# Experts of at most 64 tokens: both parts of the activations side by side in one weight tile, and a block's places by one instruction

## The chip, the cores and the metric

The kernel runs on one core of one Trainium2 chip. The metric is the device time of one execution in microseconds (us), given as the median of several runs. In the profile the engines are PE (TensorE, the matrix products), PEld (TensorE loading its weights, which overlaps PE), DVE (VectorE), ACT (ScalarE), POOL (GpSimd) and SP (SyncE, which issues most transfers). Matrix results land in PSUM, in banks of 128 rows by 512 float32; everything else is in SBUF.

## What is computed

The program is two blocks of a network on 512 tokens of 1024 features, all in float32. The change touches one stage of the first block, the mixture of experts:

```python
expert_id = grp_idx * EXPERTS_PER_GROUP + top_idx      # two of 16 experts per token
for e in range(N_EXPERTS):
    h = jax.nn.silu(t @ w_e_gate[e]) * (t @ w_e_up[e])  # 1024 -> 512
    y = y + comb[:, e:e + 1] * (h @ w_e_down[e])        # 512 -> 1024
```

The 512 tokens choose 1024 places in all, so an expert has 64 tokens on average; how many it has depends on the inputs.

## The kernel before

**Experts in an order.** The kernel computes only the tokens that chose an expert. It sorts 14 of the 16 experts by size at run time and works on them in a fixed order of places e = 0 to 15. `RANKS` (line 62) gives the rank by size that stands at each place, and `SIZES` (line 63) the rows that a block of each rank gets: places 0 to 4 have 128 rows, 5 and 6 have 96, 7 and 8 have 80, 9, 10, 12 and 13 have 64, 14 and 15 have 48. Places 4 and 11 (`DOUBLE`) have a second block of 128 rows that shares the weights: 18 blocks in all.

**Float32 by three passes.** TensorE takes float32 here in an exact split, a high part and a low part. `mm3` (line 519) makes a term of a product by three passes: high by high, high by low, low by high. In the experts the activations are the stationary operand (128 features by the block's rows) and the weights stream past, 512 columns a pass. Each pass has its own line: 522 (high activations, high weights), 523 (high activations, low weights), 524 (low activations, high weights).

```python
mm(ps, lhsT=lhsT[0], rhs=rhs[0], start=first, stop=False)
mm(ps, lhsT=lhsT[0], rhs=rhs[1], start=False, stop=False)
mm(ps, lhsT=lhsT[1], rhs=rhs[0], start=False, stop=last)
```

**Weights.** An expert has 12 chunks of 128 by 1024 weights (512 KB), four each for gate, up and down. `Stream` loads them ahead from SP (line 213), ScalarE copies the high part (`whi`, line 275), and VectorE subtracts to get the low part (`wlo`, line 283). One chunk in twelve, and a few more, have the low part made by GpSimd (`pool_lo`). There are four pairs of tiles for parts, so the split runs at most three chunks ahead of the products. After the products of a chunk, `advance` (line 318) issues the split of the chunk three places on.

**One step of the loop (line 1958).** For expert e the order on TensorE is: gate of e (`rows_mm`, 8 terms, one bank), down of e - 1 (`down`, 4 terms by two banks), up of e (`rows_mm`, 8 terms). A block thus takes 24 + 24 + 24 = 72 passes. Beside them:
- `hidden` (line 1659), after the up product: ScalarE takes silu of the gate's bank (line 1663), VectorE multiplies it with the up bank (line 1664).
- `next_h`, in the next gate: the hidden rows are transposed (line 1331) and split by `parts_T` (line 1628), high part by ScalarE (line 1638), low part by VectorE (line 1639), into two tiles `hl`. `next_x`, in the up phase, does the same with the gathered tokens of the next expert.
- at the end of `down` (line 1667), ScalarE copies each of two banks to `ye` (line 1689), GpSimd multiplies by a row, `gt_f` (line 1690), and GpSimd issues the transfer to memory (line 1692). The last expert's two banks are multiplied by VectorE straight from PSUM instead (line 1687), and SP sends the rows.
- in chunk 0 of the up phase, `pre_prep` makes the one-hot matrix of the block two blocks on: `one_hots` (line 1527) compares a row of 0, 1, 2, ... with the tokens' places, one instruction for each of four tiles of tokens (line 1531). In chunk 3, `prep` turns it into a list of tokens and gathers their rows by an indirect transfer from GpSimd (line 1548).

Each engine takes its instructions in the order in which they are issued here. `first_max`, `order`, `places` and the norm of a memory tensor (`memory_parts`) run as tasks beside the products, in the same queues. After the last `down` the rows are gathered back (line 2057) and a second norm and the second block follow; that part is not changed.

Of the kernel before, what the change touches and what calls it, by code (L numbers as in the profile page):

```python
# [20 lines left out]
NT = 4  # L21
# [19 lines left out]
# The experts in the order of their work: two stand still, and the two largest of the others come  # L41
# at places where two blocks of tokens share the weights.
# [17 lines left out]
# By the place in that order: the rank by size of its expert, and the rows of its (first) block. Of  # L60
# the others, the k-th largest has 1024 / k tokens at most; what is beyond a block is computed too.
RANKS = (-1, -1, 2, 3, 0, 4, 5, 6, 7, 8, 9, 1, 10, 11, 12, 13)
SIZES = (128, 128, 128, 128, 96, 96, 80, 80, 64, 64, 64, 64, 48, 48)
# [102 lines left out]
class Stream:  # L166
    """Chunks of weights in the order of their use: loads run ahead, then each chunk is cut
    exactly into a high and a low part of float32r."""
# [90 lines left out]
    def prepare(self):  # L259
        """What is done first to the chunks that are loaded."""  # L260
# [3 lines left out]
    def split_hi(self):  # L264
        """The high part of the next chunk."""
# [12 lines left out]
    def split_lo(self):  # L278
        """The low part, after the high one."""
# [28 lines left out]
    def take_raw(self, key):  # L308
        """A chunk as it is."""
# [8 lines left out]
    def advance(self, late=False):  # L318
        """Called after the products of a chunk: the parts of a later one."""
# [15 lines left out]
class Steps:  # L335
    """Instructions that depend on one another, put in the order in which the engines could start
    them: an engine takes its instructions in the order of their emission."""
# [6 lines left out]
    def add(self, engine, us, fn, deps=(), at=0.0, late=0.0):  # L344
        """us: about how long it holds its engine; at: not before; late: gives way to others."""
# [31 lines left out]
class Kern:  # L377
# [49 lines left out]
    def act_view(self, act, q, h):  # L427
        """Tiles 4h .. 4h + 3 of a part as one tile [128, 4, 512]."""
# [17 lines left out]
    def rsqrt(self, out, in_, premul, eps, n, p=128):  # L446
        """out = (in_ * premul + eps) ** -0.5 by Newton's steps from a guess of the exponent."""
# [30 lines left out]
    def steps_rsqrt(self, steps, z, dep, scale, eps, h0, late=0.0):  # L478
        """(z["ss"] * scale + eps) ** -0.5 of [128, 1] in z["r"], in steps after dep."""
# [21 lines left out]
    def log1p_exp_neg_abs(self, out, x, n, p=128):  # L501
        """out = log(1 + exp(-|x|)), by the series of the inverse hyperbolic tangent."""
# [16 lines left out]
    def mm3(self, ps, lhsT, rhs, first, last):  # L519
        """One term of a float32 product: three passes over exact parts."""  # L520
# [5 lines left out]
    def proj_T(self, ps, w, m0, act, nk, k0=0, every=0):  # L526
        """ps[128 features, 512 tokens] = w[:, :, m0:m0+128].T @ act, over nk tiles of rows."""
# [7 lines left out]
    def step(self, n=1):  # L535
        """Emit the next part of every task that runs beside the products."""
# [144 lines left out]
    def times_gt(self, t, n):  # L681
        """The columns of the mix's last product times 1 + gt_m."""
# [5 lines left out]
    def row_tiles(self, names):  # L688
        """The four tiles of rows [128, 1024]."""
# [3 lines left out]
    def first_mixer(self):  # L693
# [18 lines left out]
        # silu(c)  # L712
# [6 lines left out]
        # normalised x, transposed  # L719
# [27 lines left out]
        # the first two modulations by feature, a half of each by products, a half by sums  # L747
# [83 lines left out]
        # block-diagonal weights of the gates  # L831
# [20 lines left out]
        # ---- forget gates: cum of log_sigmoid along the tokens, rows of heads  # L852
# [5 lines left out]
        def forget(ps):  # L858
# [19 lines left out]
            # sums along the tokens, rows of heads  # L878
# [17 lines left out]
        # ---- recurrent branch  # L896
# [65 lines left out]
        # squares summed over the features, by half; the scales of their rows  # L962
# [3 lines left out]
        def mixed(nm, m, src, hl):  # L966
            """Tile m of a half of the features is ready."""
# [32 lines left out]
        # ---- attention, two heads after the others  # L1000
# [31 lines left out]
        # ---- the projections  # L1032
# [60 lines left out]
        # the experts' rows; those of blocks that may not be computed are cleared  # L1093
# [37 lines left out]
        # the experts' rows; those of blocks that may not be computed are cleared  # L1131
# [2089 lines left out]
```

## Time and profile before

| what | value |
|---|---|
| time before, median of 3 runs | 2381.77 us (2377.67 to 2387.61) |
| profiled execution: span, first to last instruction | 2380.5 us |
| own time of the profiled execution | none is given beside its span |
| PE busy | 2253.2 us (95%) |
| DVE busy | 1494.7 us (63%) |
| ACT busy | 1164.1 us (49%) |
| POOL busy | 435.0 us (18%) |
| stage of the experts, first pass to last | 380.7 to 745.3 us |

The span is a profile of one execution. Matrix passes are pipelined: a pass of 512 columns is shown as about 400 ns long, but the next one starts some 230 ns later, so the busy time of PE counts overlaps once and hides short waits. The pace of passes is read from their starts.

### The profile page before, as it was taken

Reading aid. Unit: us, or ns where it says so; the run is one execution under the profiler, and the core shown is the slowest. Engines: PE = TensorE matmul, PEld = TensorE weight load, DVE = VectorE, ACT = ScalarE, POOL = GpSimd, SP = SyncE. Lnnn points to the kernel's source line nnn. Section 1 sums busy time; section 2 is a strip of 40 time slices with the busy share of each in tenths; the row PEclk is TensorE's granted clock in tenths of the full one; section 3 lists DMA queues with packets and bytes.
Section 4 is the critical chain, followed back from the end, with each engine's and each line's share of the span. In section 5 each row is a group of like instructions: output and inputs, shape, how many; then the busy total and the mean of one; then the engine's idle time right before and its main releaser. Section 6 shows DMA issues by size and latency. Waiting matters only on the chain.

```text
span 2380.5 us, 29945 instructions
## 1 busy us (share of the span) xinstructions
PE 2253.2 (95%) x10972; PEld 1765.8 (74%) x10972; DVE 1494.7 (63%) x2536; ACT 1164.1 (49%) x2018; POOL 435.0 (18%) x341
## 2 busy tenths in 40 slices
PE   7789787998997899999999999999999999999998
PEld 4566466775665777778888888888777788888887
DVE  7845677989887855546567665256554566666623
ACT  5565444766675654444354443246544435444421
POOL 2464323444444411100000000011110000000000
PEclk9999897998999899999999999999999999999999
DMA  9553237989988332213333333222321232333331
GB/s 298 157 177 99 98 115 257 357 302 300 312 279 267 90 91 78 87 56 100 95 89 98 97 98 112 92 86 83 94 87 53 83 115 71 106 98 98 107 97 62
DMA packets 298091, 323.77 MB, mean 136 GB/s; under 512 B 10976, under 2 KB 216816, under 8 KB 297936
## 3 DMA queue, kind: packets, MB, share of 16 engines
q1 hardware_dynamic: 285904, 281.77, 37.5%
q0 software_dynamic: 12032, 40.00, 5.1%
q8 instruction: 88, 1.44, 0.3%
q14 instruction: 67, 0.55, 0.1%
HBM read 305.15 MB, written 16.52 MB: 135 GB/s over the span
## 4 chain that ended last, share of the span: by engine, by line
PE 62%; DVE 4%; ACT 2%; issue 1%; DMA 0%; DVEq 0%; ACTq 0%; POOLq 0%
PE ps L522 19%; PE ps L524 18%; PE ps L523 18%; PE ps L2398 2%; PE ps L2564 1%; PE ps L591 1%; PE ps L2582 1%; DVE wlo L283 1%; ACT g L2977 1%; PE ps L2563 1%; PE ps L2683 1%; DVE st L494 0%; DVE x L2956 0%; DMA y<-y_d,si 0%; PE ps L2528 0%
## 5 line engine op out<-in xcount | busy, mean ns | idle before, releaser
L283 DVE TENSOR_TENSOR wlo<-wraw,whi 128x1024 fp32r<-128x1024 f32 (+1 forms) x337 | 430.6, 1281 | 351.0 <-ACT whi L275 180.8
L522 PE MATMUL ps<-hT,whi 128*128 128x512 f32 x1280 | 514.4, 402 | 0.0
L524 PE MATMUL ps<-hT,wlo 128*128 128x512 f32 x1280 | 499.7, 390 | 0.0
L523 PE MATMUL ps<-hT,whi 128*128 128x512 f32 x1280 | 499.3, 390 | 0.0
L275 ACT ACTIVATE whi<-wraw 128x1024 fp32r<-128x1024 f32 (+1 forms) x346 | 360.2, 1048 | 212.5 <-DVE wlo L283 146.7
L522 PEld LDWEIGHTS ps<-hT,whi 128*128 128x128 f32 x1280 | 240.3, 188 | 63.7 <-issue 7.4
L524 PEld LDWEIGHTS ps<-hT,wlo 128*128 128x128 f32 x1280 | 240.2, 188 | 52.2
L523 PEld LDWEIGHTS ps<-hT,whi 128*128 128x128 f32 x1280 | 240.6, 188 | 45.6
L522 PE MATMUL ps<-whi,hi 128*128 128x512 f32 x480 | 189.5, 395 | 0.0
L524 PE MATMUL ps<-whi,lo 128*128 128x512 f32 x480 | 189.1, 394 | 0.0
L523 PE MATMUL ps<-wlo,hi 128*128 128x512 f32 x480 | 189.0, 394 | 0.0
L523 PE MATMUL ps<-wlo,hl 128*128 128x512 f32 (+4 forms) x432 | 175.6, 406 | 9.7 <-DVE wlo L283 4.9
L522 PE MATMUL ps<-whi,hl 128*128 128x512 f32 (+4 forms) x432 | 177.7, 411 | 0.4 <-ACT hl L1638 0.4
L524 PE MATMUL ps<-whi,hl 128*128 128x512 f32 (+4 forms) x432 | 173.8, 402 | 2.5 <-DVE hl L1639 2.5
L283 DVE TENSOR_TENSOR wlo<-wx,whi 128x1024 fp32r<-128x1024 f32 x107 | 147.0, 1396 | 15.2 <-ACT whi L275 13.2
L275 ACT ACTIVATE whi<-wx 128x1024 fp32r<-128x1024 f32 x121 | 125.7, 1057 | 40.4 <-PE ps L523 27.3
L596 ACT ACTIVATE gr<-ps 128x256 fp32r<-128x256 f32 (+2 forms) x128 | 49.1, 384 | 182.0 <-PE ps L591 181.4
L599 DVE TENSOR_TENSOR gr<-ps,gr 128x256 fp32r<-128x256 f32 (+2 forms) x128 | 53.9, 421 | 119.6 <-ACT gr L596 119.1
L524 PEld LDWEIGHTS ps<-whi,lo 128*128 128x128 f32 x480 | 90.1, 188 | 21.3
L523 PEld LDWEIGHTS ps<-wlo,hi 128*128 128x128 f32 x480 | 90.2, 188 | 21.0
L522 PEld LDWEIGHTS ps<-whi,hi 128*128 128x128 f32 x480 | 90.1, 188 | 20.9
L523 PEld LDWEIGHTS ps<-wlo,hl 128*128 128x128 f32 (+4 forms) x432 | 71.7, 166 | 45.8 <-DVE wlo L283 10.9
(509 smaller groups left out, 3993.7 us busy)
## 6 DMA issues: line engine op xcount, KB each, us to landing
wraw<-in_w_in_dram SPq DMA_DIRECT2D x108, 512.0 KB, 3.9
wraw<-in_w_up_dram SPq DMA_DIRECT2D x88, 512.0 KB, 3.8
wx<-in_w_e_down_dram SPq DMA_DIRECT2D x46, 512.0 KB, 4.9
wraw<-in_w_down_dram SPq DMA_DIRECT2D x44, 512.0 KB, 3.6
wx<-in_w_e_gate_dram SPq DMA_DIRECT2D x39, 512.0 KB, 5.5
wx<-in_w_e_up_dram SPq DMA_DIRECT2D x36, 512.0 KB, 6.9
ada<-in_w_ada_dram SPq DMA_DIRECT2D x32, 512.0 KB, 4.8
wraw<-in_w_e_up_dram SPq DMA_DIRECT2D x28, 512.0 KB, 8.1
```

The source lines that it names most:

```text
L275: self.k.nc.scalar.activation(out=hi[:, 0:n_el], in_=t[:, 0:n_el], func=AF.Copy)
L283: eng.tensor_tensor(out=lo[:, 0:n_el], in0=t[:, 0:n_el], in1=hi[:, 0:n_el].bitcast(F32), op=OP.subtract)
L522: mm(ps, lhsT=lhsT[0], rhs=rhs[0], start=first, stop=False)
L523: mm(ps, lhsT=lhsT[0], rhs=rhs[1], start=False, stop=False)
L524: mm(ps, lhsT=lhsT[1], rhs=rhs[0], start=False, stop=last)
L591: nc.tensor.transpose(pt_ps[:, c * 128:(c + 1) * 128], p[:, c * 128:(c + 1) * 128], self.const("ident"))
L596: nc.scalar.activation(out=hi, in_=pt_ps[:, 0:n], func=AF.Copy)
L599: nc.vector.tensor_tensor(out=lo, in0=pt_ps[:, 0:n], in1=hi.bitcast(F32), op=OP.subtract)
L2398: self.nc.tensor.matmul(ps[q][:, c], lhsT=ws[q][w][:, k, :], rhs=act()[t][k][:, c], start=(j == 0 and k == 0), stop=(j == 2 and k == KD - 1))
L2563: nc.tensor.matmul(ps, lhsT=q[e][:, c], rhs=view(k[e]), start=True, stop=False)
L2564: nc.tensor.matmul(ps, lhsT=q[e][a, c], rhs=view(k[2])[a], start=False, stop=True)
L2582: nc.tensor.matmul(ps[:, 128 * c:128 * c + 128], lhsT=lhs(view)(q, i)[64 * e:64 * e + 64], rhs=view(k, s_)[64 * e:64 * e + 64], start=True ...
```

## The change

- Ranks 12 and 13 get 64 rows in place of 48, so that places 9, 10, 12, 13, 14 and 15 all have exactly 64 rows (`PACKED`).
- For a block of 64 rows `parts_T` writes the low part beside the high part, into columns 64 to 127 of one tile of 128. `term` then takes two passes in place of three: the whole tile of 128 columns by the high weights (the results of the high part land in rows 0 to 63 of the bank, those of the low part in rows 64 to 127), and its first 64 columns by the low weights (into rows 0 to 63). The first term issues the wide pass first, the others issue it second.
- The two halves of a bank are added by `folded`: ScalarE copies rows 64 to 127 to SBUF, VectorE adds rows 0 to 63. That is done for the gate's bank, the up bank and the two banks of `down`.
- The gate of a packed expert is folded and put through silu (`gated`) in chunk 1 of the `down` between its gate and its up phase; for other experts silu stays after the up phase.
- `one_hots` makes the four tiles by one tensor_tensor with broadcast operands, in place of four tensor_scalar.

Comments were also taken out; that changes no instruction. The diff, cut to its core:

```diff
-SIZES = (128, 128, 128, 128, 96, 96, 80, 80, 64, 64, 64, 64, 48, 48)
+SIZES = (128, 128, 128, 128, 96, 96, 80, 80, 64, 64, 64, 64, 64, 64)
+PACKED = 64
...
-            for i in range(NT):
-                v.tensor_scalar(t[:, i, :], self.const("iota")[:, 0:n], col_of(i), None,
-                                op0=OP.is_equal)
+            v.tensor_tensor(out=t, in0=self.const("iota")[:, None, 0:n].to_broadcast([128, NT, n]),
+                            in1=col_of().to_broadcast([128, NT, n]), op=OP.is_equal)
...
+            if packed:
+                to = [hl[0][:, :, 0:r], hl[0][:, :, r:2 * r]]
...
+        def term(ps, x, k, w, first, last):
+            if len(x) > 1:
+                self.mm3(ps, [p[:, k, :] for p in x], w, first, last)
+                return
+            mm = nc.tensor.matmul
+            if first:
+                mm(ps, lhsT=x[0][:, k, :], rhs=w[0], start=True, stop=False)
+            mm(ps[0:PACKED], lhsT=x[0][:, k, 0:PACKED], rhs=w[1], start=False, stop=False)
+            if not first:
+                mm(ps, lhsT=x[0][:, k, :], rhs=w[0], start=False, stop=last)
...
+        def folded(ps, out=None):
+            t = self.g()[0:PACKED] if out is None else out
+            nc.scalar.activation(out=t, in_=ps[PACKED:2 * PACKED], func=AF.Copy)
+            v.tensor_tensor(out=t, in0=ps[0:PACKED], in1=t, op=OP.add)
+            return t
...
+        def gated(pg, packed):
+            if packed:
+                sg = folded(pg)
+                nc.scalar.activation(out=sg, in_=sg, func=AF.Silu)
+                return sg
...
+        def hidden(sg, pu, packed=False):
+            h = folded(pu) if packed else self.g()[0:int(pu.shape[0])]
+            v.tensor_tensor(out=h, in0=sg, in1=h if packed else pu, op=OP.mult)
...
+                if c == 1 and mid is not None:
+                    mid()
...
+                    if two:
+                        folded(py[n], ye[:, c])
+                    if at_end:
+                        v.tensor_tensor(out=ye[:, c], in0=ye[:, c] if two else py[n], in1=gt[:, c],
+                                        op=OP.mult)
```

## Rows read from the trace of the kernel before

**Rows 1.** The page's first line: the span.
```profile
span 2380.5 us, 29945 instructions
```

**Rows 2.** Busy time by stretch, one row for an expert's gate, down, up: e3, e9 to e14.
```profile
core 0: us, PE busy (x) PEld busy (x) DVE busy (x) ACT busy (x) POOL busy (x), PEclk, DMA share, GB/s
439.07:459.38 20.31, 19.64 (x101) 15.79 (x100) 19.88 (x25) 16.21 (x21) 9.48 (x5) 1.00 1.02 377
...
580.91:602.98 22.07, 19.89 (x90) 11.47 (x88) 19.57 (x21) 14.90 (x20) 11.95 (x6) 0.92 0.95 340
602.98:623.80 20.82, 19.82 (x101) 11.84 (x100) 19.44 (x25) 16.00 (x20) 11.24 (x6) 1.00 1.00 343
623.80:654.16 30.36, 29.96 (x138) 22.04 (x136) 23.30 (x28) 15.41 (x20) 14.01 (x9) 1.00 0.90 287
654.16:678.34 24.18, 24.18 (x117) 16.93 (x116) 17.61 (x19) 16.73 (x22) 9.92 (x7) 1.00 0.80 244
678.34:696.41 18.07, 18.07 (x85) 10.32 (x84) 16.64 (x16) 14.53 (x18) 9.08 (x7) 1.00 0.95 317
696.41:714.59 18.18, 18.18 (x86) 9.71 (x85) 16.99 (x17) 14.03 (x18) 8.07 (x4) 1.00 0.86 288
```

**Rows 3.** The same view: gate of e15 and down of e14, up of e15, down of e15.
```profile
714.59:726.19 11.60, 11.60 (x53) 6.08 (x52) 10.63 (x10) 9.20 (x12) 2.82 (x1) 1.00 1.02 360
726.19:737.59 11.40, 6.37 (x29) 3.30 (x28) 7.72 (x6) 7.96 (x17) 8.70 (x7) 0.89 0.62 170
737.59:745.28 7.69, 7.69 (x26) 3.91 (x27) 6.37 (x14) 4.61 (x5) 0.00 (x0) 0.72 0.82 270
```

**Rows 4.** Timeline of PE where e11's 128 columns of weights give way to e12's 64.
```profile
653.92 0.39 PE L524 MATMUL ps<-whi,hl 128*128 128x512 f32 x1
654.16 0.40 PE L522 MATMUL ps<-whi,hl 128*64 128x512 f32 x1
654.39 0.39 PE L523 MATMUL ps<-wlo,hl 128*64 128x512 f32 x1
```

**Rows 5.** Groups of instructions by shape, 380 to 780 us: busy, mean ns.
```profile
L1664 DVE TENSOR_TENSOR g<-g,ps 64x512 f32<-64x512 f32 x4 | 2.7, 671 | 0.0
L1689 ACT ACTIVATE ye<-ps 64x512 f32<-64x512 f32 x8 | 4.4, 580 | 0.2
L1531 DVE TENSOR_SCALAR oh<-const,pp 128x64 f16<-128x64 f32 x16 | 5.0, 379 | 0.0
```

**Rows 6.** Timeline of DVE and POOL around e13's up phase; the second column is the duration.
```profile
689.37 5.69 DVE L283 TENSOR_TENSOR wlo<-wx,whi 128x1024 fp32r<-128x1024 f32 x3
690.33 3.65 POOL L1690 TENSOR_TENSOR ye<-ye,gt_f 64x512 f32<-64x512 f32 x2 [4.23 <-ACT ye L1689]
...
697.78 1.21 DVE L283 TENSOR_TENSOR wlo<-wraw,whi 128x1024 fp32r<-128x1024 f32 x1
698.92 0.67 DVE L1664 TENSOR_TENSOR g<-g,ps 64x512 f32<-64x512 f32 x1
```

**Rows 7.** The same view in e12's up phase: one-hots, splits of transposes, GpSimd's products.
```profile
670.50 3.11 POOL L1690 TENSOR_TENSOR ye<-ye,gt_f 128x512 f32<-128x512 f32 x2 [10.07 <-ACT ye L1689]
671.12 2.85 DVE L1531 TENSOR_SCALAR oh<-const,pp 128x48 f16<-128x48 f32 x4
674.58 1.68 POOL L1690 TENSOR_TENSOR ye<-ye,gt_f 128x512 f32<-128x512 f32 x1
675.02 0.74 DVE L1639 TENSOR_TENSOR hl<-ps,hl 128x256 fp32r<-128x256 f32 x2
```

**Rows 8.** Timeline of DVE in the up phase of e0, before the first result rows.
```profile
399.15 0.87 DVE L1531 TENSOR_SCALAR oh<-const,pp 128x128 f16<-128x128 f32 x4
```

**Rows 9.** Timeline of PE in the second block: passes of 128 rows and of 64 rows.
```profile
841.50 0.36 PE L2563 MATMUL ps<-gr 128*128 128x256 f32 x1
841.79 0.38 PE L2564 MATMUL ps<-gr 64*128 64x256 f32 x1
842.10 0.50 PE L522 MATMUL ps<-hT,whi 128*128 128x512 f32 x1
```

More of the change, by code (lines that the diff above doesn't have):

```diff
@@ L1589, in routing @@
             v.tensor_scalar(posm, posm, 1.0, None, op0=OP.subtract)
-            oh = one_hots(lambda i: posm[:, i, 0:1])
+            oh = one_hots(lambda: posm[:, :, 0:1])
             yield
@@ L1630, in parts_T @@
             r = int(src.shape[0])
+            packed = r == PACKED
             if n == 4:
-                hl = [self.gen.tile([128, n, 128], F32R, tag="g", name="hl") for _ in range(2)]
-            else:
-                hl = [w4.tile([128, n, 128], F32R, tag=tg, name="hl", bufs=N_XT) for tg in tags]
-            hl = [t[:, :, 0:r] for t in hl]
+                hl = [self.gen.tile([128, n, 128], F32R, tag="g", name="hl")
+                      for _ in range(1 if packed else 2)]
+            else:
+                hl = [w4.tile([128, n, 128], F32R, tag=tg, name="hl", bufs=N_XT)
+                      for tg in tags[0:1 if packed else 2]]
@@ L1636, in parts_T @@
+            if packed:
+                to = [hl[0][:, :, 0:r], hl[0][:, :, r:2 * r]]
+            else:
+                hl = to = [t[:, :, 0:r] for t in hl]
             for h in range(n // 4):
                 p3 = self.transposes(src, h)
-                nc.scalar.activation(out=hl[0][:, 4 * h:4 * h + 4, :], in_=p3, func=AF.Copy)
-                v.tensor_tensor(out=hl[1][:, 4 * h:4 * h + 4, :], in0=p3,
-                                in1=hl[0][:, 4 * h:4 * h + 4, :].bitcast(F32), op=OP.subtract)
@@ L1641, in parts_T @@
-            return hl
+                nc.scalar.activation(out=to[0][:, 4 * h:4 * h + 4, :], in_=p3, func=AF.Copy)
+                v.tensor_tensor(out=to[1][:, 4 * h:4 * h + 4, :], in0=p3,
+                                in1=to[0][:, 4 * h:4 * h + 4, :].bitcast(F32), op=OP.subtract)
+            return hl
+        def term(ps, x, k, w, first, last):
[8 more added lines that the diff above has]
+                mm(ps, lhsT=x[0][:, k, :], rhs=w[0], start=False, stop=last)
@@ L1643, in rows_mm, with bank @@
+        def bank(x):
+            return self.psA()[0:int(x[0].shape[2])]
+        def folded(ps, out=None):
[3 more added lines that the diff above has]
+            return t
         def rows_mm(xTs, nm, e, take, mid={}):
-            pss = [self.psA()[0:int(xT[0].shape[2])] for xT in xTs]
+            pss = [bank(xT) for xT in xTs]
@@ L1651, in rows_mm @@
                         k = 2 * c + kk
-                        self.mm3(ps, [p[:, k, :] for p in xT], [p[:, kk, :] for p in w], k == 0,
-                                 k == 7)
+                        term(ps, xT, k, [p[:, kk, :] for p in w], k == 0, k == 7)
                 if take == W.take:
@@ L1657, in rows_mm, with down @@
             return pss
-        def hidden(pg, pu):
-            r = int(pg.shape[0])
-            sg = self.g()[0:r]
-            h = self.g()[0:r]
+        def gated(pg, packed):
[3 more added lines that the diff above has]
+                return sg
+            sg = self.g()[0:int(pg.shape[0])]
             nc.scalar.activation(out=sg, in_=pg, func=AF.Silu)
-            v.tensor_tensor(out=h, in0=sg, in1=pu, op=OP.mult)
-            return h
-        def down(hTs, e, take, rows_to):
-            pys = [[self.psA()[0:int(hT[0].shape[2])] for _ in range(2)] for hT in hTs]
+            return sg
+        def hidden(sg, pu, packed=False):
+            h = folded(pu) if packed else self.g()[0:int(pu.shape[0])]
+            v.tensor_tensor(out=h, in0=sg, in1=h if packed else pu, op=OP.mult)
+            return h
+        def down(hTs, e, take, rows_to, mid=None):
+            pys = [[bank(hT) for _ in range(2)] for hT in hTs]
+            packed = [len(hT) == 1 for hT in hTs]
             for c in range(4):
+                if c == 1 and mid is not None:
+                    mid()
                 w = take(("w_e_down", e, c))
@@ L1673, in down @@
                     for n in range(2):
-                        self.mm3(py[n], [p[:, c, :] for p in hT],
-                                 [p[:, 512 * n:512 * n + 512] for p in w], c == 0, c == 3)
+                        term(py[n], hT, c, [p[:, 512 * n:512 * n + 512] for p in w], c == 0, c == 3)
                 if take == W.take:
@@ L1679, in down @@
             for row in rows_to:
-                py = pys.pop(0)
-                r = int(py[0].shape[0])
+                py, two = pys.pop(0), packed.pop(0)
+                r = PACKED if two else int(py[0].shape[0])
                 ye = w4.tile([128, 1024], F32, tag="ye", name="ye")[0:r]
                 gt = rows["gt_f"][0:r]
+                at_end = W.pos == W.limit and take == W.take
                 for n in range(2):
                     c = slice(512 * n, 512 * n + 512)
-                    if W.pos == W.limit and take == W.take:
-                        v.tensor_tensor(out=ye[:, c], in0=py[n], in1=gt[:, c], op=OP.mult)
+                    if two:
[3 more added lines that the diff above has]
+                                        op=OP.mult)
                         continue
-                    nc.scalar.activation(out=ye[:, c], in_=py[n], func=AF.Copy)
+                    if not two:
+                        nc.scalar.activation(out=ye[:, c], in_=py[n], func=AF.Copy)
                     nc.gpsimd.tensor_tensor(out=ye[:, c], in0=ye[:, c], in1=gt[:, c], op=OP.mult)
@@ L1812, in first_moe @@
             if e < N_STATIC:
-                cols.append(lambda i, e=e: posm[:, i, e:e + 1])
+                cols.append(lambda e=e: posm[:, :, e:e + 1])
             else:
-                cols.append(lambda i, e=e: pp[:, i, e:e + 1])
+                cols.append(lambda e=e: pp[:, :, e:e + 1])
             if e in DOUBLE:
                 blocks[-1].append(len(cols))
-                cols.append(lambda i, d=DOUBLE.index(e): pd[d][:, i, :])
+                cols.append(lambda d=DOUBLE.index(e): pd[d])
                 sizes.append(128)
@@ L1962, in first_moe, with gates_done @@
             pg = rows_mm([xT[n] for n in blocks[e]], "w_e_gate", e, W.take, mid)
+            sg = {}
+            def gates_done():
+                for n in blocks[e]:
+                    if n not in sg:
+                        sg[n] = gated(pg.pop(0), sizes[n] == PACKED)
             if e:
                 down([h.pop(n) for n in blocks[e - 1]], e - 1, W.take,
-                     [block_row[n] for n in blocks[e - 1]])
+                     [block_row[n] for n in blocks[e - 1]],
+                     gates_done if sizes[blocks[e][0]] == PACKED else None)
             if e == MEM_E:
@@ L1976, in first_moe @@
             pu = rows_mm([xT.pop(n) for n in blocks[e]], "w_e_up", e, W.take, mid)
-            for n, g, u in zip(blocks[e], pg, pu):
-                h[n] = hidden(g, u)
-            del g, u, pg, pu
+            gates_done()
+            for n in blocks[e]:
+                h[n] = hidden(sg.pop(n), pu.pop(0), sizes[n] == PACKED)
+            del pg, pu
             if e == 6:
@@ L2020, in first_moe @@
             pc, at[NE + j] = choose(j)
-            oT = parts_T(gather(token_list(one_hots(lambda i: pc[:, i, :])),
+            oT = parts_T(gather(token_list(one_hots(lambda: pc)),
                                 w4.tile([128, 1024], F32, tag="xg", name="xg")),
@@ L2044, in first_moe @@
             pu = rows_mm([oT], "w_e_up", 0, take)
-            down([parts_T(hidden(pg[0], pu[0]), 4)], 0, take, [START[NE] + 128 * j])
+            down([parts_T(hidden(gated(pg[0], False), pu[0]), 4)], 0, take, [START[NE] + 128 * j])
             del pg, pu, oT, W2, t
```

## The prediction

> **What bounds the kernel now.** The change touches only the stage of the experts, 365 of the 2380.5 us of the profiled span [rows 1]. I first cut that stage into one stretch per expert and read the busy time of every engine in each, because an average over the stage mixes experts with different limits. The reader is to see three kinds of stretch [rows 2, 3]. With a second block of 128 tokens (e11 by itself, e12 because e11's down falls into it) PE never rests and VectorE is idle for 7.1 of 30.4 and 6.6 of 24.2 us: PE alone sets the time. In e13, e14 and the first part of e15 PE has no gap, but VectorE is also busy for 16.64 of 18.07, 16.99 of 18.18 and 10.63 of 11.60 us. In e9 and e10 VectorE is busy for 19.57 of 22.07 and 19.44 of 20.82 us, and there the stretch is longer than PE's work: 72 passes at the pace of 0.23 us [rows 4] are 16.6 us, to which some 1.5 us of transposes come (e13, without a gap, takes 18.07). So e9 and e10 already wait for VectorE, and e13 to e15 have two limits that lie within 1.5 us of each other.
>
> Then I looked at why VectorE is so full, in the timeline of VectorE and GpSimd side by side. A low part takes 1.21 us undisturbed, but three in a row took 5.69 us while two of GpSimd's products ran [rows 6]: the two engines took turns, and VectorE paid GpSimd's time on top of its own. The splits that read PSUM are not held up: two took 0.74 us together in the middle of a GpSimd product [rows 7]. VectorE's true load in a stretch is therefore its own work plus nearly all of GpSimd's.
>
> **The change, part by part.**
>
> *Passes.* Six experts are packed: e9, e10, e12, e13, e14, e15. Each saves 8 of 24 passes in gate, in up and in down, so 144 in all. A pass of 64 columns of weights keeps the pace of one of 128 (0.24 us from the wide to the narrow, 0.23 after it [rows 4]), so PE is spared 8 × 0.23 = 1.84 us per phase, 33.1 us in all. That is worth its full price only where PE alone is the limit.
>
> *Change of width.* The new passes alternate between 128 and 64 columns, which the old stage does only at the border of two experts. There it costs nothing that shows [rows 4]. At most it could cost what a change of height costs: between a pass of 128 rows and one of 64 rows 0.29 and 0.31 us passed for 256 columns [rows 9], against the half of 0.23 that 256 columns need, so 0.18 us more. From below: no gain is to be had, since every pass streams 512 columns either way. I take 0, since the border is the nearer row: same engine, same stage, columns changed. The Trainium skill, TensorEngine Tiling (Array Packing), section Tiling Modes, says that a change of the tiling mode drains TensorE; if passes of 64 columns count as another mode, the sum would have the 0.18 us at every alternation. That rule is weighed as a rival below; the border row speaks against its applying here.
>
> *Folds.* A packed expert has four: gate, up and two banks of down, 24 in all. Each is a ScalarE copy (0.58 us as in the copies to `ye` [rows 5]) and a VectorE addition of 64 × 512 from PSUM and SBUF. The product with the up bank has just these operands: 0.67 us [rows 5], but low parts of 1.21 us start 1.14 us apart [rows 6], as an instruction starts some 0.07 us before the one ahead of it ends; I take 0.60. So VectorE gets 24 × 0.60 = 14.4 us more. Because the addition reads PSUM, it can run while GpSimd holds VectorE's other work up [rows 7]; I allow 0.5 us of such overlap per packed expert. ScalarE gets some 14 new copies, 8.1 us; it is busy for 14 to 16 of 18 to 22 us in these stretches [rows 2], which covers them. If that cover went, each copy would cost its 0.58 us.
>
> *What waits behind the folds.* VectorE waits in its queue for ScalarE's copy, and that for the last pass of the phase; behind it stand the next low parts. The low part issued before the fold is already three chunks ahead of PE, and the next one needs a tile that PE frees at that same last pass, so VectorE would wait there anyway; I cost this at 0. GpSimd's product with `gt_f` now starts 0.6 us later; it has idle time of 6 us and more per stretch [rows 2].
>
> *One-hots.* Four comparisons take 0.87 us when GpSimd is quiet [rows 8] and 2.85 us when two of its products are running [rows 7]. One instruction of 256 elements should cost a quarter of the 1.21 us of 1024, about 0.3 us, with 0.6 us for 512 elements. The 2 us of waiting do not go away: if the comparison is over sooner, the next low part meets GpSimd's product in its place. So 0.2 to 0.3 us per block are saved from below, 2.3 us from above (0.87 - 0.6 and 2.85 - 0.6). I take the lower end, as the low parts of rows 6 wait in the same way.
>
> *Larger blocks.* e14 and e15 have 64 rows in place of 48: four splits grow by under 0.1 us each, and the gathers by 16 rows. Costed at 0.
>
> **The sum by stretch** (limit after the change: what is larger of PE's work and VectorE's load plus about 0.5 us of idle time that no queue avoids):
> - e1 to e8: VectorE is at the limit in some, such as e3 (19.88 of 20.31 [rows 2]); 0.2 to 0.3 us of one-hots in four or five of them: **-1.0**.
> - e9: VectorE 19.57 + 1.2 (gate and up folded) - 0.2 = 20.6, and about 1 of its 2.5 us idle stays, because it no longer waits for PE as much: 21.6, **-0.5**.
> - e10: 19.44 + 2.4 - 0.5 (two one-hots) - 0.5 (overlap) + 0.4 = 21.2, **+0.4**.
> - e11: PE is the limit, e10's down loses 8 passes: **-1.8**.
> - e12: gate and up lose 16: **-3.7**, to 20.5; VectorE, 17.61 + 1.2, still fits.
> - e13: PE falls to about 12.6, VectorE sets it: 16.64 + 2.4 - 0.6 + 0.4 = 18.8, **+0.8**. e14: 16.99 + 2.4 - 0.6 + 0.4 = 19.2, **+1.0**.
> - e15's gate and e14's down: 10.63 + 1.8 = 12.4, **+0.8**. e15's up, where ScalarE and GpSimd already keep PE waiting (6.37 of 11.40 [rows 3]): a copy and an addition more on the way to the hidden rows, **+1.2**.
> - e15's down and the last rows: 8 passes fewer, at a granted clock of 0.72 [rows 3] about 0.23 us each or more, -1.8; a copy and two additions more before the rows leave, +1.2: **-0.6**.
>
> Together -3.4 us: 2377.1 for the profiled execution, whose own time is known only as its span. The median of the runs lies 1.3 us above that span, so against it I get 2381.8 - 3.4 = 2378.4.
>
> **The rivals.**
> 1. *VectorE's whole addition is paid* (slower). The place is the head start of the low parts, three chunks. If e12's quicker phases use it up, e11 and e12 do not shorten, and all 14.4 us of folds less 1 us of one-hots come on top: 2395. It decides from the point at which VectorE's 7.1 and 6.6 us of idle time in e11 and e12 cannot be moved to e13. For it: VectorE is nearly full on both sides [rows 2]. Against it: PE's passes in e11 leave VectorE more time than it needs. Chance 0.09.
> 2. *Every alternation drains* (slower). A packed expert has 14 alternations per phase, 252 in six experts; at 0.18 us, 48 passes and 42 changes take 18.6 us where 72 passes took 16.6: +12, 2394. Chance 0.04. By the skill's rule on tiling modes this would be the outcome; no run here shows that alternation within an expert.
> 3. *The waits of the one-hots vanish* (faster). If GpSimd's products fall into gaps instead, 2 us are saved in up to five stretches at VectorE's limit, 10 in all: 2368. Against it: low parts took turns with GpSimd in rows 6. Chance 0.09.
> 4. *PE's passes set the pace everywhere* (faster): -33, 2349. For it: PE has no gap from e11 to e14 [rows 2]. Against it: VectorE's busy time there. Chance 0.05.
> 5. *The new passes do less than said*, say wide passes wait for their 128 columns of weights and nothing is spared: 2382. Chance 0.03.
>
> **How the numbers follow.** The forecast has 0.70. A measurement of this kernel can tell about 0.5% from no change, 11.9 us: faster is below 2369.9, slower above 2393.7. Cases 3 (most of it) and 4 are faster, and a little of the forecast's own spread: 0.15. Cases 1 and 2 are slower, with little of that spread: 0.13. The rest is 0.72. The forecast's own range, from its bounds (folds without overlap +3, no shortening of e12 +4, stalls of the fold in e15 +2; one-hots at twice the gain -3, tail -2, e9 at PE's pace -3), is 2370 to 2388. To leave out no more than 2 in 10, I reach to cases 1 and 3 at their near ends: 2367 to 2393.
>
> **What would show it right or wrong.** Right: in the packed stretches PE has gaps, ended by VectorE's low parts, VectorE is busy for over 95% in e13 and e14, e11 and e12 are 1.8 and 3.7 us shorter, and passes of both widths start 0.23 us apart. One instruction in place of four comparisons shows about 0.3 to 0.6 us when undisturbed, and one wait of about 1 us for GpSimd. Wrong: e13 and e14 well below 17 us would say that VectorE had room; a start-to-start of 0.4 us at the change of width would say that TensorE drains; a granted clock near 0.5 in e13 to e15, because PE rests more often, would say that slower passes take back what fewer passes gave.

## The result, and the profile after

The changed kernel takes 2396.59 us (median, 2392.69 to 2401.88), the kernel before 2382.2 us on the same chip: a ratio of 1.006, with an interval of 1.0041 to 1.008. It is slower, by 14.4 us. The forecast was 2378.4 us, the range ended at 2393, and slower had a chance of 0.13.

The first lines of the page of after:

```profile
span 2400.1 us, 29650 instructions
## 1 busy us (share of the span) xinstructions
PE 2234.9 (93%) x10828; PEld 1760.0 (73%) x10828; DVE 1507.8 (63%) x2506; ACT 1171.5 (49%) x2032; POOL 448.3 (19%) x341
```

PE has 144 passes fewer and is 18.3 us less busy than before, yet the span is 19.6 us longer than the one of [rows 1]. The profiled execution is the longest of those measured (2401.88 us), and it comes to the first pass of an expert 5.8 us later than the one of before (386.52 against 380.7 us). In the profiles of the experiments with the same early part that pass comes at 379.9 to 383.7 us, so I set those 5.8 us aside as a matter of this one execution. What is left, 13.8 us, agrees with the medians. Those starts lie up to 3.8 us apart, so below a verdict rests on ratios, and only the place of a loss on a profile.

Busy time by stretch in the profile of after, the columns as in [rows 2]: e9 to e14, then, as in [rows 3], gate of e15 with down of e14, up of e15, down of e15.

```profile
586.58:610.15 23.57, 18.14 (x73) 10.61 (x72) 20.92 (x20) 15.19 (x20) 11.86 (x6) 0.88 0.96 320
610.15:632.60 22.45, 17.53 (x78) 11.11 (x76) 20.14 (x21) 16.64 (x22) 12.16 (x5) 0.90 0.86 303
632.60:661.66 29.06, 28.11 (x129) 21.44 (x128) 24.24 (x29) 16.15 (x22) 16.03 (x11) 1.00 0.98 304
661.66:682.19 20.53, 20.53 (x102) 15.67 (x100) 15.56 (x16) 16.46 (x22) 7.97 (x7) 1.00 0.87 267
682.19:703.62 21.43, 14.78 (x61) 7.76 (x60) 19.14 (x21) 15.36 (x21) 10.67 (x5) 1.00 0.86 288
703.62:727.60 23.98, 15.26 (x62) 8.86 (x60) 19.97 (x20) 16.02 (x21) 17.13 (x6) 0.86 0.68 228
727.60:741.37 13.77, 9.72 (x37) 4.67 (x35) 11.46 (x12) 8.38 (x12) 5.25 (x3) 1.00 0.97 312
741.37:756.18 14.81, 5.49 (x21) 2.77 (x21) 12.29 (x12) 10.43 (x19) 9.67 (x7) 0.84 0.42 124
756.18:762.64 6.46, 6.46 (x18) 4.34 (x19) 5.20 (x12) 4.38 (x6) 0.00 (x0) 0.58 0.98 322
```

Each length less the one of [rows 2, 3] gives the sum of the prediction term by term:

| stretch | forecast | measured |
|---|---|---|
| e1 to e8 (179.32 us before, 179.36 after) | -1.0 | 0.0 |
| e9 | -0.5 | +1.5 |
| e10 | +0.4 | +1.6 |
| e11 | -1.8 | -1.3 |
| e12 | -3.7 | -3.7 |
| e13 | +0.8 | +3.4 |
| e14 | +1.0 | +5.8 |
| gate of e15, down of e14 | +0.8 | +2.2 |
| up of e15 | +1.2 | +3.4 |
| down of e15, and its rows | -0.6 | +1.0 (-1.2 and +2.2) |
| sum | -3.4 | +13.9 |

The gains are where they were forecast. The losses are in the stretches where they were forecast (and in e9), but 17.9 us in place of 4.2. And they are not VectorE's work alone: in e13 and e14 VectorE is busy for 19.14 of 21.43 and 19.97 of 23.98 us. That is 2.5 and 3.0 us more work than before, but its rests grew too, from 1.4 and 1.2 us to 2.3 and 4.0, while PE rests for 6.7 and 8.7. No engine is full in these two stretches, so engines wait for one another.

The view of the waits says which ones. Its columns are: who waited for whom, us in total, how often, the longest. Before, from the first pass of e9 to the last of e15:

```profile
DVE wlo L283 <- ACT whi L275: 14.6, 20, 1.9
...
ACT whi L275 <- DVE wlo L283: 4.6, 4, 1.5
PEld ps L523 <- POOL wlo L283: 4.4, 4, 2.5
PEld ps L523 <- DVE wlo L283: 3.0, 6, 0.8
```

After, in the same part:

```profile
POOL ye L1733 <- DVE ye L1671: 39.0, 5, 8.6
PEld ps L1660 <- DVE wlo L285: 26.3, 33, 2.0
DVE wlo L285 <- ACT whi L277: 18.1, 18, 1.7
...
ACT g L1692 <- DVE g L1671: 15.3, 6, 4.3
PE ps L1660 <- DVE wlo L285: 13.2, 20, 2.0
...
PEld ps L1660 <- POOL wlo L285: 9.5, 4, 5.9
```

ScalarE's silu of a packed gate (line 1692) waited for VectorE's addition in all six packed experts, 15.3 us in all. Before, ScalarE waited for VectorE for 4.6 us there, in four high parts (line 275). At the same time VectorE waits longer for high parts (18.1 us for 14.6), and PE much longer for low parts of VectorE and of GpSimd.

One such place, in e13's gate and the `down` after it, from the timeline of after (start, duration; the time in brackets is idle time before):

```profile
691.02 3.51 DVE L285 TENSOR_TENSOR wlo<-wx,whi 128x1024 fp32r<-128x1024 f32 x2 [0.61 <-ACT whi L277]
...
691.97 0.59 ACT L1670 ACTIVATE g<-ps 64x512 f32<-64x512 f32 x1
...
694.46 0.68 DVE L1671 TENSOR_TENSOR g<-ps,g 64x512 f32<-64x512 f32 x1
...
695.16 0.63 ACT L1692 ACTIVATE g<-g 64x512 f32<-64x512 f32 x1 [2.60 <-DVE g L1671]
...
695.70 1.99 ACT L277 ACTIVATE whi<-wx 128x1024 fp32r<-128x1024 f32 x2
696.77 1.23 DVE L285 TENSOR_TENSOR wlo<-wx,whi 128x1024 fp32r<-128x1024 f32 x1 [1.65 <-ACT whi L277]
...
696.80 0.50 PE L1659 MATMUL ps<-whi,hl 128*128 128x512 f32 x1 [1.04 <-ACT whi L277]
```

It is to be read as a chain through two queues. ScalarE's copy of the bank ends at 692.56. The addition that it allows stands behind two low parts in VectorE's queue and starts at 694.46. ScalarE's next instruction is the silu of that sum, so ScalarE stands still for 2.60 us, with the next high parts behind it. When the silu is done, VectorE has run out of high parts and rests for 1.65 us, and so does PE, for 1.04. Each of the two engines has waited for the other once.

GpSimd's part, from the timeline of after, from e13's up phase to the `down` after e14's gate (that gate begins at 703.62):

```profile
700.94 13.43 POOL L1733 TENSOR_TENSOR ye<-ye,gt_f 64x512 f32<-64x512 f32 x2 [8.63 <-DVE ye L1671]
...
705.45 1.22 DVE L285 TENSOR_TENSOR wlo<-wraw,whi 128x1024 fp32r<-128x1024 f32 x1
...
706.58 0.68 DVE L1671 TENSOR_TENSOR g<-ps,g 64x512 f32<-64x512 f32 x1
...
713.17 0.68 DVE L1671 TENSOR_TENSOR g<-ps,g 64x512 f32<-64x512 f32 x1
...
715.27 2.37 POOL L285 TENSOR_TENSOR wlo<-wx,whi 128x1024 fp32r<-128x1024 f32 x1
...
717.69 0.69 PE L1660 MATMUL ps<-wlo,hl 128*64 128x512 f32 x1 [5.46 <-POOL wlo L285]
```

The two products with `gt_f`, which took 3.65 us together in [rows 6], take 13.43. The next computation in GpSimd's queue is a low part of weights. ScalarE's copy for it ended at 708.53, but it starts at 715.27, 6.7 us later, when the products and the transfer behind them are through, and PE waits for it for 5.46 us. After that rest seven passes start 0.43 us apart in place of 0.23, and the granted clock of the stretch is 0.86, where [rows 2] have 1.00.

### The profile page after: what moved, and what is told of

Read it like the earlier page. It is cut to its first block, busy times and chain, and to the rows that moved or that the text cites. A ratio compares the mean times of both kernels' runs of the same rounds, so it can differ in the third digit from the quotient of the medians.

```text
span 2400.1 us, 29650 instructions
## 1 busy us (share of the span) xinstructions
PE 2234.9 (93%) x10828; PEld 1760.0 (73%) x10828; DVE 1507.8 (63%) x2506; ACT 1171.5 (49%) x2032; POOL 448.3 (19%) x341
## 4 chain that ended last, share of the span: by engine, by line
PE 61%; DVE 4%; ACT 2%; issue 1%; DMA 0%; DVEq 0%; POOL 0%; ACTq 0%; POOLq 0%; another core or an unknown queue 0%
PE ps L524 19%; PE ps L526 18%; PE ps L525 18%; PE ps L2450 2%; PE ps L2616 1%; PE ps L593 1%; PE ps L2634 1%; DVE wlo L285 1%; ACT g L3029 1%; PE ps L2615 1%; PE ps L2735 1%; DVE st L496 0%; DVE x L3008 0%; DMA y<-y_d,si 0%; PE ps L2580 0%
## 5 line engine op out<-in xcount | busy, mean ns | idle before, releaser
L285 DVE TENSOR_TENSOR wlo<-wx,whi 128x1024 fp32r<-128x1024 f32 x107 | 152.3, 1445 | 16.9 <-ACT whi L277 13.8
L525 PE MATMUL ps<-wlo,hl 128*128 128x512 f32 (+2 forms) x288 | 117.8, 409 | 9.8 <-DVE wlo L285 7.2
L524 PE MATMUL ps<-whi,hl 128*128 128x512 f32 (+2 forms) x288 | 119.4, 415 | 0.0
L526 PE MATMUL ps<-whi,hl 128*128 128x512 f32 (+2 forms) x288 | 116.8, 405 | 2.7 <-DVE hl L1647 2.6
L525 PEld LDWEIGHTS ps<-wlo,hi 128*128 128x128 f32 x480 | 90.2, 188 | 20.9
L524 PEld LDWEIGHTS ps<-whi,hi 128*128 128x128 f32 x480 | 90.1, 188 | 20.9
L3092 ACT ACTIVATE g<-ps,small 128x512 f32<-128x512 f32 x88 | 68.1, 774 | 61.7 <-PE ps L526 61.7
```

The source lines that it names most:

```text
L285: eng.tensor_tensor(out=lo[:, 0:n_el], in0=t[:, 0:n_el], in1=hi[:, 0:n_el].bitcast(F32), op=OP.subtract)
L3092: nc.scalar.activation(out=c, in_=ps, func=AF.Identity, scale=w[1], bias=self.small("conv_b2", 44 * l + tile_))
```

## The experiments

My theory (A) was that the order of instructions costs most: silu's wait for an addition that is queued behind low parts. Its rivals: that the additions are simply paid (B), and that GpSimd's late products and low parts are the cost (C). All times are medians, and each ratio is to the kernel before on the same chip.

**Silu of the gate after the up phase.** The fold stays in `down`, only the silu moves; no work is removed.

```diff
         def gated(pg, packed):
             if packed:
-                sg = folded(pg)
-                nc.scalar.activation(out=sg, in_=sg, func=AF.Silu)
-                return sg
+                return folded(pg)
...
         def hidden(sg, pu, packed=False):
+            if packed:
+                nc.scalar.activation(out=sg, in_=sg, func=AF.Silu)
```

> The changed kernel, but silu of a packed gate is issued after the up phase, not right behind its fold. Theory A (ScalarE stands still: its silu waits for VectorE's addition, 15.3 us in six waits in the profile of the changed kernel, and VectorE then waits some 1.6 us each time for the next high part): those waits go, and with them 6 x 1.6 = 10 us of VectorE's; 2385 to 2389 against 2396.6. Theory B (VectorE's 24 additions of 0.6 us are the whole loss): unchanged within 2 us, 2395 to 2398. Theory C (GpSimd comes too late with its low parts): unchanged or 1 to 2 us better.

Measured: 2387.96 us, 1.0031 (1.002 to 1.0042), that is 0.29% or 6.9 us less than the change as it was made; with both intervals some 2 to 12 us. The group of the six silus in this kernel (busy, mean ns, idle time before) has no idle time any more:

```profile
L1698 ACT ACTIVATE g<-g 64x512 f32<-64x512 f32 x6 | 3.7, 620 | 0.0
```

About half of the loss is thus the place of one ScalarE instruction. In the same part of this profile VectorE waits 14.3 us for high parts, about as much as before the change. PE's weight loads still wait 27.3 us for VectorE's low parts, so those waits do not come from the place of silu.

**No folds.** The passes and the one-hots of the change, without the copies and additions; rows 64 to 127 of the banks are left unread, so the low part of the activations times the high weights is missing from the result.

```diff
-                sg = folded(pg)
-                nc.scalar.activation(out=sg, in_=sg, func=AF.Silu)
+                sg = self.g()[0:PACKED]
+                nc.scalar.activation(out=sg, in_=pg[0:PACKED], func=AF.Silu)
...
-                    if two:
-                        folded(py[n], ye[:, c])
...
-                    if not two:
-                        nc.scalar.activation(out=ye[:, c], in_=py[n], func=AF.Copy)
+                    nc.scalar.activation(out=ye[:, c], in_=py[n][0:r], func=AF.Copy)
```

> The changed kernel with its two passes and one-hots, but without the folds: rows 64 to 127 of the packed banks are left out of gate, up and down, and the instructions after them read rows 0 to 63 as before the change. What the passes alone bring. Theory B: 14.4 us of VectorE and its waits go, and e11 and e12 keep their 5 us: 2376 to 2380. Theory A expects as much, since no silu waits for VectorE here either. A rival that the narrower stretches of passes cost time by themselves (clock, order of widths): 2388 or more.

Measured: 2378.95 us, 0.999 (0.998 to 0.9999). The folds with all that hangs on them are therefore worth 0.70%, 16.7 us; the 33.1 us of passes that they pay for are worth 2.4 (0.2 to 4.8), one-hots included. e13 and e14 of this kernel, by stretch:

```profile
674.22:693.58 19.36, 14.48 (x62) 7.71 (x60) 18.73 (x17) 14.51 (x19) 11.99 (x7) 1.00 1.01 322
693.58:711.70 18.12, 14.45 (x62) 7.73 (x60) 18.12 (x16) 14.32 (x19) 7.66 (x4) 1.00 0.83 275
```

VectorE never rests in e14, and the two stretches together take 37.48 us, where they took 36.25 before, with 48 passes fewer and no folds. The same view for the low parts of weights alone in these two stretches; first the kernel before:

```profile
678.34:714.59 36.25, 30.84 (x23) 5.44 (x2) 1.00 0.90 303
```

Then without folds:

```profile
674.22:711.70 37.48, 34.03 (x23) 6.10 (x2) 1.00 0.92 299
```

VectorE made 23 low parts each time, in 30.84 us and in 34.03 us. VectorE's busy time was no fixed load. All low parts of over 1.3 us there, seven before and eight here, run beside a computation of GpSimd, and the time that the two overlap grew from 11.1 to 16.3 us. That they meet more often because PE no longer holds them apart is my reading; no run changes that alone.

**One-hots alone.** The kernel before, with the one tensor_tensor in place of four comparisons (the diff is the one shown with the change).

> The kernel before with the one-hots by one instruction, and no packing. All theories: 0.2 to 0.3 us of VectorE per block where it is at its limit, 2380 to 2382. If the waits of the four comparisons for GpSimd vanish (rival 3 of the prediction): 2370 to 2374.

Measured: 2380.2 us, 0.9992 (0.9982 to 1.0002), not told apart from no change; rival 3 with its 2368 us is out.

**Low parts of `w_e_down` by VectorE.** In e8 to e14 the low part that GpSimd makes goes to VectorE, so that no low part of weights stands behind the products with `gt_f`.

```diff
-    return (nm, c) == ("w_e_down", 1) or (nm, e, c) in MORE or (nm, e, c, *_) in KV_POOL
+    return ((nm, c) == ("w_e_down", 1) and not 8 <= e <= 14 or (nm, e, c) in MORE
+            or (nm, e, c, *_) in KV_POOL)
```

> The changed kernel, but the low part of the second chunk of down of e8 to e14 is made by VectorE and not by GpSimd. Theory C (TensorE waits for GpSimd's low parts, up to 5.5 us in e13's down): 2386 to 2391. Theory B (VectorE is the limit): seven low parts of 1.14 us more on VectorE, less the 7 x 2.35 us of GpSimd's time that it no longer pays: between 2388 and 2400. Theory A: within 3 us of 2396.6.

Measured: 2388.42 us, 1.0029 (1.0019 to 1.0038), as C expected, though still inside the wide range of B. VectorE, the engine nearest to its limit, got seven more low parts of 1.21 us, and the kernel still became 0.31% or 7.4 us faster (some 2 to 13). The products stay as slow: in e14 of this kernel GpSimd is busy for 15.18 us with four instructions, but nobody waits for them.

```profile
694.45:714.30 19.85, 14.22 (x61) 8.01 (x60) 18.17 (x21) 15.44 (x21) 15.18 (x4) 1.00 0.78 262
```

**Both remedies at once**, to see if these are two costs or one.

> Both remedies at once: silu issued late (alone 2388.0) and the low parts of down by VectorE (alone 2388.4), against 2396.6 for the change. If ScalarE's standing still and GpSimd's lateness are two losses that do not touch: 2396.6 - 8.6 - 8.2 = 2380. If they are one chain (silu late, so high parts late, so GpSimd late) that either remedy cuts: 2386 to 2389.

Measured: 2385.03 us, 1.0018 (1.0009 to 1.0027). Had the two been independent, 0.60% would have gone; 0.42% went. The intervals together leave some 0.26% either way, so the times alone do not tell one chain from two costs. The profiles speak for a link. First the pair of products for e12's rows with the silu late, then the same pair with the low parts by VectorE and the silu still early:

```profile
689.81 3.50 POOL L1733 TENSOR_TENSOR ye<-ye,gt_f 64x512 f32<-64x512 f32 x2 [6.89 <-DVE ye L1671]
```

```profile
691.77 14.57 POOL L1734 TENSOR_TENSOR ye<-ye,gt_f 64x512 f32<-64x512 f32 x2 [12.92 <-DVE ye L1672]
```

With the silu late, alone or with both remedies, a pair of 64 rows takes 3.50 to 5.14 us; with it early there is one of 13.43 in the change and two of 14.57 in this second kernel. So in these profiles the long pairs go with the early silu; how the one makes the other is not shown. What is left over the kernel without folds is 0.28%, 6.7 us, with the seven low parts that VectorE took over in it.

**Each addition twice**, on top of both remedies, the first one into a spare tile.

```diff
             nc.scalar.activation(out=t, in_=ps[PACKED:2 * PACKED], func=AF.Copy)
+            spare = self.g()[0:PACKED]
+            v.tensor_tensor(out=spare, in0=ps[0:PACKED], in1=t, op=OP.add)
+            del spare
             v.tensor_tensor(out=t, in0=ps[0:PACKED], in1=t, op=OP.add)
```

> The kernel with both remedies (2385.0), but each of the 24 additions of a fold is done twice, the first into a spare tile that nothing reads: the price of an addition where nothing else is moved. If VectorE is the limit wherever they stand: 24 x 0.6 = 14.4 us, 2399. If a part of them runs while GpSimd holds the other work up, as the prediction allowed (0.5 us per packed expert): 2396. If they hide beside TensorE: 2385 to 2389.

Measured: 2395.26 us, 1.0055 (1.0038 to 1.0072). That is 0.37% or 8.8 us over the kernel above, with the two intervals some 4 to 13 us, for 24 additions: about 0.37 us each, of the 0.60 at which they were priced. In this profile VectorE is busy for 21.31 of 21.65 us in e13 and 20.84 of 21.07 in e14: behind the waits it is the limit, and part of each addition seems to be covered. The doubled addition also makes the way to the hidden rows longer, which this run doesn't hold apart.

**The whole gate after the up phase**, its fold too (`mid` is None, as for experts that aren't packed). If an addition between ScalarE's instructions did harm wherever it stands, this would not help.

> The change, but the gate's fold and silu are issued after the up phase, as silu was before the change. The chain copy, addition, silu, copy, addition, product then stands in one place. If what counts is that ScalarE's silu waits for VectorE's addition, at whatever place: no better than the change, 2394 to 2399. If it was the place in the middle of down that did harm: 2386 to 2390, as with silu late.

Measured: 2389.96 us, 1.0037 (1.0025 to 1.005): 0.23% better than the change, which only just clears the intervals (some 0 to 0.46%). It agrees with the second expectation: the harm comes from the place in the middle of `down`, where low parts are queued. It is not better than moving silu alone; in its profile the part from e15's gate to its up phase takes 31.5 us, against 26.9 with silu alone moved, since there the whole chain of the hidden rows comes after the last pass.

**Products with `gt_f` by VectorE**, with the late silu, for packed experts.

```diff
-                at_end = W.pos == W.limit and take == W.take
+                at_end = two or W.pos == W.limit and take == W.take
```

> The change with silu late (2388.0), and the product of a packed expert's result rows with their factor by VectorE, not GpSimd: ten products fewer on GpSimd (1.2 us each, which VectorE paid while it was full), ten more of 0.6 us on VectorE. If GpSimd's time is what VectorE waits for: 10 x 0.6 = 6 us better, 2381 to 2384. If GpSimd only took VectorE's idle time: 6 us worse, 2393 to 2395.

Measured: 2388.4 us, 1.0031 (1.002 to 1.0042), the same as with the late silu alone, and neither of the values expected. With the late silu GpSimd's products were not slow any more (3.50 to 5.14 us a pair), so there was less to gain than expected; VectorE's ten additional products and the end of GpSimd's cancel, and this run doesn't price either by itself.

**Only e12 packed**, and **only e10 and e12 packed**, where e11's 144 passes or e12's own lie beside the spared ones and PE alone is the limit. The other places of rank 8 and beyond get 72 or 48 rows, which keeps them at three passes; silu stands late.

```diff
-SIZES = (128, 128, 128, 128, 96, 96, 80, 80, 64, 64, 64, 64, 64, 64)
+SIZES = (128, 128, 128, 128, 96, 96, 80, 80, 72, 64, 64, 72, 48, 48)
```

(That is e10 and e12; for e12 alone the tenth size is 72 too.)

> Packing only in e12, whose gate and up stand beside a double block; the other blocks of 64 have 72 rows and take three passes, silu late, one-hots by one instruction. By the accounts of the profile (e12's stretch 24.18 before, 20.53 after) 3.7 us are won there, and two folds fall into e13's stretch at VectorE's limit, 1.2 us: 2380.2 - 3.7 + 1.2 = 2377.7. If e13 loses as much as with all packed (3.4 us): 2380.

> As e6, but e10 packed too: its down falls into e11, where TensorE is the limit (1.8 us won), its gate and up into e10, where VectorE is (two folds, 1.2 us, less what TensorE's quicker phase gives there). 2376 to 2379 if the losses are as counted; 2381 or more if e10 loses the 1.6 us that it lost with all packed.

Measured: 2379.07 us, 0.999 (0.9981 to 0.9999), with e12 packed; 2377.09 us, 0.9982 (0.9973 to 0.9991), with both. The first lies between the two values expected, the second where it was expected. The second is faster than either kernel of this case, by 0.18% and by 0.78%; with the same late silu and all six packed the ratio was 1.0031. Its stretches e10, e11 and e12:

```profile
605.16:624.11 18.95, 16.68 (x86) 10.50 (x84) 18.36 (x20) 15.41 (x20) 12.56 (x5) 1.00 0.98 344
624.11:652.24 28.13, 28.09 (x129) 21.39 (x128) 23.32 (x28) 16.86 (x23) 17.39 (x11) 1.00 1.00 332
652.24:672.52 20.28, 20.28 (x102) 15.60 (x100) 15.10 (x16) 15.64 (x21) 7.75 (x7) 1.00 0.80 265
```

They take 18.95, 28.13 and 20.28 us, against 20.82, 30.36 and 24.18 in [rows 2]: 8.0 us gained, of which e13 gives back 2.5 (20.58 us in place of 18.07).

## Why the prediction was wrong, and where it was right

**Right: where passes are worth their price.** e11 and e12 became 1.3 and 3.7 us shorter, forecast 1.8 and 3.7. e12's gain is steady: 20.3 to 20.9 us in the profiles of the experiments that pack it. e11's is not: against 30.36 us before it took 28.13 with two places packed, but 29.75 already with the one-hots alone, 30.63 with the silu late at a granted clock of 0.94, and 31.80 with the whole gate after the up phase at 0.89. Low parts end most of PE's waits in the packed stretches, as foretold, but VectorE is busy there for 89% and 83% (e13, e14) and not for over 95%: beside its work its rests had grown. Of 33.1 us of passes, the run without folds shows 2.4 in the time. Rivals 4 (PE everywhere) and 3 (waits of one-hots) are out.

**Right: a change of width costs nothing.** Passes of 128 and 64 columns by turns, in e12 of after (timeline of PE):

```profile
662.36 0.39 PE L1662 MATMUL ps<-whi,hl 128*128 128x512 f32 x1
662.58 0.39 PE L1660 MATMUL ps<-wlo,hl 128*64 128x512 f32 x1
662.82 0.39 PE L1662 MATMUL ps<-whi,hl 128*128 128x512 f32 x1
663.04 0.39 PE L1660 MATMUL ps<-wlo,hl 128*64 128x512 f32 x1
```

Starts are 0.22 to 0.24 us apart in both directions, the pace of [rows 4], so rival 2 falls; rival 5 falls with the 3.7 us that e12 gave. By the rule of the Trainium skill, TensorEngine Tiling (Array Packing), section Tiling Modes, a change of mode drains TensorE; the trace shows no drain here, so fewer columns of weights alone are no change of mode in that sense, as far as these rows reach.

**Wrong: "What waits behind the folds", costed at 0.** I followed VectorE's queue (it waits for ScalarE's copy) and did not follow ScalarE's: the silu waits for VectorE's sum, with high parts of weights behind it. I named idle time as the cover, but ScalarE stood still for 15.3 us in front of six silus, with high parts of weights queued behind them. It cost 6.9 us by the run that moves silu alone, and some 10 us together with the low parts that GpSimd made late.

**Wrong: GpSimd's later product, costed at 0 because GpSimd "has idle time".** The step counted a start 0.6 us later. One pair of products took 13.43 us, with a low part that PE needs behind it; the other eight products took 17.0 us together, 2.1 each, against 1.87 before, so the mean of 3.07 below is mostly that one pair. Moving the low parts to an engine with less room gained 7.4 us. Groups of after (busy, mean ns, idle time before):

```profile
L1733 POOL TENSOR_TENSOR ye<-ye,gt_f 64x512 f32<-64x512 f32 x10 | 30.5, 3066 | 39.0 <-DVE ye L1671 39.0
...
L1671 DVE TENSOR_TENSOR g<-ps,g 64x512 f32<-64x512 f32 x12 | 8.1, 676 | 0.0
...
L1700 DVE TENSOR_TENSOR g<-g 64x512 f32<-64x512 f32 x6 | 7.1, 1191 | 0.2
```

**Mis-sized: VectorE's load.** The sum took VectorE's busy time of [rows 2] (16.64 us in e13) and added folds to it. That time had been measured where PE paced the work; without folds it was 18.73 us at once, and 23 equal low parts grew by 3.2 us. The prediction said that VectorE pays GpSimd's time too, and then took that time into the sum as it had been before. A second part was not seen: the product in `hidden`, 671 ns with an operand in PSUM [rows 5], now has both operands in SBUF and takes 1191 ns in the mean, 3.1 us over six experts. The additions, which read PSUM, took 676 ns, as the row that they were priced by. The mean of the product mixes two cases. Where no computation of GpSimd ran beside it, as in e14, it took 0.68 us (three of six); where one did, 1.07, 1.91 and 2.12 us, the last in e15:

```profile
731.70 0.68 DVE L1700 TENSOR_TENSOR g<-g 64x512 f32<-64x512 f32 x1
```

```profile
752.32 2.12 DVE L1700 TENSOR_TENSOR g<-g 64x512 f32<-64x512 f32 x1
```

The Trainium skill, SBUF — State Buffer, section Who interferes with whom, says that a VectorE instruction with two SBUF inputs contends with a GpSimd instruction that reads SBUF. The trace agrees: 0.68 us alone and up to 2.12 beside GpSimd for the product with two SBUF inputs, 676 ns in the mean for the addition that reads a bank.

**Mis-sized: the tail.** A copy and two additions before the last rows were put at 1.2 us. From the last pass to the transfer of the rows it was, before:

```profile
744.87 0.40 PE L524 MATMUL ps<-whi,hl 128*48 128x512 f32 x1
...
747.40 0.34 SPq L1692 DMA_DIRECT2D y_d<-ye  x1
```

and after:

```profile
762.24 0.39 PE L1662 MATMUL ps<-whi,hl 128*128 128x512 f32 x1
...
766.26 0.68 DVE L1728 TENSOR_TENSOR ye<-ye,gt_f 64x512 f32<-64x512 f32 x1
...
766.97 0.53 SPq L1735 DMA_DIRECT2D y_d<-ye  x1
```

2.53 us became 4.73: two copies, then addition and product by turns, 2.2 us more, and the rest of the program is just as much later. The 8 passes spared in e15's down gave 1.2 and not 1.8 us, at a granted clock of 0.58 where [rows 3] have 0.72: most of them start 0.43 us apart.

**One-hots.** Each was put at 0.2 to 0.3 us of gain. The one instruction is about as long as forecast, 0.41 us for 256 elements and 0.69 for 512 undisturbed, up to 1.79 beside GpSimd's products. Alone they bring 0.08% of 2382, 1.9 us, with no gain at all inside the interval.

**Rival 1** named 2395 us, near what came, for another reason. It had VectorE's head start used up in e12, so that e11 and e12 would not shorten; they did. Its time came right by luck, its mechanism did not.

What stays open: how the 6.7 us that remain with both remedies split among additions, product, tail and the low parts that VectorE took over; the doubled additions bound the first at 4 to 13 us.

## What to carry to other kernels

A saving on the engine that looks busiest is worth its price only in the stretches where no other engine is close behind: packing two places of six beat packing all six, with the same late silu by 0.49%. When work moves to other engines, follow each engine's queue in order, and look for an instruction that waits for an engine whose answer is itself queued; here one ScalarE instruction between two of VectorE's cost about 6.9 us, and idle time elsewhere did not cover it. A busy time read under one bottleneck is not a load that can be added to under another, above all where two engines slow each other down.

## What the runs showed that was not expected

Two GpSimd products of 64 by 512 took 13.43 us together (6.88 and 6.59) while VectorE had one low part after another ready, against 3.65 in [rows 6], where a turn each was the rule. VectorE's low parts beside them took 1.21 to 1.22 us each, as long as undisturbed, so here GpSimd did nearly all of the waiting. The first product ended 1.2 us after the start of an addition that reads PSUM, and so did the second, as if GpSimd had waited for a VectorE instruction that leaves it room; but splits that read PSUM ran at 702.52 as well, and the first product did not end there. Such a pair came again twice with the low parts by VectorE (14.57 us each), and one of 8.10 with the whole gate after the up phase. Who gets its turn when, and why, was not tried by itself and stays open.
